# An encoder block on one core: who puts the tokens of the neighbourhood branch into column order

## The chip, the core and the metric

The kernel runs on one core of one Trainium2 chip. A core has TensorE (PE in the profile; its weight loads are the row PEld), VectorE (DVE), ScalarE (ACT), GpSimd (POOL) and SyncE (SP, which here only issues transfers). The metric is the device time of one execution in microseconds (us), lower is better.

## The reference, cut to what matters

One layer of an encoder over 1024 tokens of width 1024. The tokens are a grid of 16 rows by 64 columns, token = 64 * row + column.

```python
proj = x @ w_in + b_in                     # columns: NA q | NA k | NA v | WG q | WG k | WG v | gate_A | gate_B
ya = neighbourhood_attention(qa, ka, va)   # 8 heads of 64; a query sees an 8 x 16 window of the grid
yb = windowed_gqa(qb, kb, vb)              # 8 q heads, 2 kv heads, |t-s| <= 128
mix = sigmoid(ga) * (ya @ w_branch_a) + sigmoid(gb) * (yb @ w_branch_b)
h   = layer_norm(alpha * x + mix @ w_out)
out = layer_norm(alpha * h + expert_choice_moe(h))   # 16 SwiGLU experts, 128 tokens each
```

In row order a query's window of 16 columns is spread over the grid rows. The kernel therefore computes branch A in *column order*, token' = 16 * column + row, where a block of 128 tokens is 8 whole columns and a window lies in at most three neighbouring blocks. Everything outside branch A stays in row order.

## The kernel before, in words

Each float32 operand is split into a high part (hi, rounded to the matmul type fp32r) and the rest (lo), and a product is hi*hi + hi*lo + lo*hi. ScalarE writes the hi part, VectorE the lo part.

The stages, one after another on TensorE, whose program is in the order of the code (`manual_schedule`):

1. **Projection and attention, mixed.** `x_tile` transposes x into x^T, held in row order as `xT`. `w_in` is cut into 34 chunks of 128 columns. `proj(c, nh)` makes chunk c for one half of the tokens (nh): 24 matmuls of 128x512 into one PSUM tile `pj` (two buffers). Chunks 0 to 3 are NA q, 4 to 7 NA k, 8 to 11 NA v; 12 to 17 belong to branch B, 18 to 33 are the gates. Units of this projection wait in a list (`queue`), and `fill(n)` puts n of their matmuls between the steps of the attention (5 or 7 at a time, `FILL`, `FILA`), in an order fixed by the program. Before a unit's first matmul TensorE waits until the buffer of `pj` used two units earlier has been emptied.
2. **Branch outputs.** The attention outputs go through memory (`ya_d` in column order, `yb_d` in row order) and are loaded, split and multiplied by `w_branch_a`, `w_branch_b` in `branch(nm, d)`: 8 chunks d, two halves nh, 12 matmuls of 128x512 each for each of the two branches. The result is gated with `g_d`.
3. **Output product, LayerNorm, router and top-128 choice**, then **16 experts** whose weights are read from memory, and the last LayerNorm.

Where the order of tokens changes in the kernel before: the matmuls read x^T in row order, so `pj` is in row order, and the evictions of chunks 0 to 11 write into column order. `by_column` is the strided view (64 bytes between neighbouring columns) through which `kside` (lines 208 and 210), `qside` (217, 218) and `va_unit` (281) write; VectorE reads the hi part back through the same view. `qa_unit` needs four pieces of 64x256 for each half of tokens, since one half of the rows holds all columns. The way back is in `y_load`: for branch A the row is read through a strided view (also 64 bytes) by ScalarE (595) and VectorE (596). The functions that the change touches, with the line numbers of the profile:

Of the kernel before, what the change touches and what calls it, by code (L numbers as in the profile page):

```python
# [8 lines left out]
F32 = mybir.dt.float32  # L9
F32R = mybir.dt.float32r  # L10
I32 = mybir.dt.int32
U32 = mybir.dt.uint32
AF = mybir.ActivationFunctionType
ALU = mybir.AluOpType
# [3 lines left out]
P = 128  # L18
S = 1024
D = 1024  # L20
KD = D // P
HD = 64
GRID = 64
# [31 lines left out]
def encoder_block(ctx, tc, x, w_in, b_in, rpb, sink, w_branch_a, w_branch_b, w_out, ln1_g, ln1_b,  # L55
                  w_router, w_gate, w_up, w_down, ln2_g, ln2_b, out):
    nc = tc.nc
# [19 lines left out]
    def f32(ap):  # L77
        return ap.bitcast(F32)
# [31 lines left out]
    xp = att.enter_context(tc.tile_pool(name="xp", bufs=1))  # L110
    tbp = att.enter_context(tc.tile_pool(name="tbp", bufs=2))
    qkv = att.enter_context(tc.tile_pool(name="qkv", bufs=1))
    vtp = att.enter_context(tc.tile_pool(name="vtp", bufs=1))
    spp = att.enter_context(tc.tile_pool(name="spp", bufs=2))
    prp = att.enter_context(tc.tile_pool(name="prp", bufs=2))
    evp = att.enter_context(tc.tile_pool(name="evp", bufs=3))
    psc = att.enter_context(tc.tile_pool(name="psc", bufs=1, space=PSUM))
    ptp = att.enter_context(tc.tile_pool(name="ptp", bufs=3, space=PSUM))
    pvp = att.enter_context(tc.tile_pool(name="pvp", bufs=1, space=PSUM))
# [2 lines left out]


    xT = {}
    for h in range(2):
        for part in ("hi", "lo"):
            xT[part, h] = xp.tile([P, KD, 512], F32R, name="xT" + part + str(h))

    def x_load(t):
        xt = qkv.tile([P, D], F32, name="xt", tag="k", bufs=6)  # L130
# [3 lines left out]
    def x_tile(xt, t):  # L134
        for h in range(2):
            pt = ptp.tile([P, 4, P], F32, name="pt")
            for j in range(4):
                nc.tensor.transpose(pt[:, j, :], xt[:, (4 * h + j) * P:(4 * h + j + 1) * P], ident)
            sl = slice((t % 4) * P, (t % 4 + 1) * P)
            dst = xT["hi", t // 4][:, 4 * h:4 * h + 4, sl]  # L140
            nc.scalar.activation(dst, pt, AF.Copy)
            nc.vector.tensor_tensor(xT["lo", t // 4][:, 4 * h:4 * h + 4, sl], pt, f32(dst), op=ALU.subtract)

    held = {}
    wq, raws = [], []
# [28 lines left out]
    bcol = acp.tile([P, 34], F32, name="bcol")  # L174
    nc.vector.tensor_copy(bcol, bps[:, 0, :34])

    def proj(c, nh):
        hi, lo = held["w", c]
        ps = pp.tile([P, 512], F32, name="pj")
        n = 0  # L180
        for a, part in ((hi, "hi"), (hi, "lo"), (lo, "hi")):
            for k in range(KD):
                nc.tensor.matmul(ps, a[:, k, :], xT[part, nh][:, k, :], start=(n == 0), stop=(n == 3 * KD - 1))  # L183
                n += 1
                yield ps

# [7 lines left out]
            nc.gpsimd.dma_start(t[:, o:o + w], src)  # L194
        return t


    def by_column(ap, nh):
        return ap.rearrange("p (c r) -> p r c", r=16)[:, 8 * nh:8 * nh + 8, :]

    def by_row(ap):
        return ap.rearrange("p (r c) -> p r c", c=GRID)

    def kside(ps, c, half, khh, kll, view, src_view):
        lo, hi = half * HD, (half + 1) * HD
        src, b = src_view(ps[lo:hi]), bcol[lo:hi, c:c + 1]
        for o in (half, 1 - half):
            nc.scalar.activation(view(khh[o * HD:(o + 1) * HD]), src, AF.Identity, bias=b)
        for o in range(2):
            nc.vector.scalar_tensor_tensor(view(kll[o * HD:(o + 1) * HD]), src, b, f32(view(khh[lo:hi])),  # L210
                                           op0=ALU.add, op1=ALU.subtract)

    def qside(src, c, half, qs, view):
        lo, hi = half * HD, (half + 1) * HD
        o = 1 - half
        b = bcol[lo:hi, c:c + 1]
        nc.scalar.activation(view(qs[lo:hi]), src, AF.Identity, bias=b)
        nc.vector.scalar_tensor_tensor(view(qs[o * HD:(o + 1) * HD]), src, b, f32(view(qs[lo:hi])),
                                       op0=ALU.add, op1=ALU.subtract)

    def k_unit(key, c, nh):
        if nh == 0:
            held[key] = ([qkv.tile([P, S], F32R, name="khh", tag="k", bufs=6) for _ in range(2)],
                         [qkv.tile([P, S], F32R, name="kll", tag="k", bufs=6) for _ in range(2)])
        for ps in proj(c, nh):
            yield
        for half in range(2):
            if key == "kB":
                v, sv = lambda ap: ap[:, nh * 512:(nh + 1) * 512], lambda ap: ap
            else:  # L230
                v, sv = lambda ap: by_column(ap, nh), by_row
            kside(ps, c, half, held[key][0][half], held[key][1][half], v, sv)
        done.add((key, nh))

    def q_unit(key, c, nh):
        for ps in proj(c, nh):
            yield
        for half in range(2):
            qs = qkv.tile([P, 512], F32R, name="qs", tag="q", bufs=8)
            held.setdefault(key, {})[half, nh] = qs  # L240
            qside(ps[half * HD:(half + 1) * HD], c, half, qs, lambda ap: ap)
        done.add((key, nh))


    def qa_unit(key, c, nh):
        if nh == 0:
            held[key] = {(half, g): qkv.tile([P, 512], F32R, name="qs", tag="q", bufs=8)
                         for half in range(2) for g in range(2)}
        for ps in proj(c, nh):
            yield  # L250
        for half in range(2):
            for g in range(2):
                src = by_row(ps[half * HD:(half + 1) * HD])[:, :, 32 * g:32 * g + 32]
                qside(src, c, half, held[key][half, g], lambda ap: by_column(ap, nh))
        done.add((key, nh))

    def v_split(key, vt, j0, last):
        pt = ptp.tile([P, 4, P], F32, name="pt")
        for j in range(4):
            nc.tensor.transpose(pt[:, j, :], vt[:, (j0 + j) * P:(j0 + j + 1) * P], ident)  # L260
        v = qkv.tile([P, 4, 2, P], F32R, name="vs", tag="v", bufs=4)
        p4 = pt.rearrange("p t (h d) -> p t h d", h=2)
        nc.scalar.activation(v[:, :, :, :HD], p4, AF.Copy)
        nc.vector.tensor_tensor(v[:, :, :, HD:], p4, f32(v[:, :, :, :HD]), op=ALU.subtract)
        held.setdefault(key, []).append(v)
        done.update(last)

    def v_unit(key, c, nh):
        for ps in proj(c, nh):
            yield  # L270
        vt = evp.tile([P, 512], F32, name="vt", tag="e")
        nc.scalar.activation(vt, ps, AF.Identity, bias=bcol[:, c:c + 1])
        later.append([8, lambda: v_split(key, vt, 0, [(key, nh)])])

    def va_unit(key, c, nh):
        if nh == 0:
            held["vt", key] = vtp.tile([P, S], F32, name="vta")
        vt = held["vt", key]
        for ps in proj(c, nh):
            yield  # L280
        nc.scalar.activation(by_column(vt, nh), by_row(ps), AF.Identity, bias=bcol[:, c:c + 1])
        if nh:
            later.append([8, lambda: v_split(key, vt, 0, [(key, 0)])])
            later.append([14, lambda: v_split(key, vt, 4, [(key, 1)])])

    def g_unit(c, nh):
        for ps in proj(c, nh):
# [31 lines left out]
    def units(f, *a):  # L319
        return [(f, a + (nh,)) for nh in range(2)]  # L320

    def qkv_units(i):
        return units(qa_unit, ("q", i), i) + units(k_unit, ("k", i), 4 + i) + units(va_unit, ("v", i), 8 + i)

    gates = [u for d in range(8) for c in (18 + d, 26 + d) for u in units(g_unit, c)]

# [261 lines left out]
    def y_load(nm, src):  # L588
        for k in range(4):
            raw = gp.tile([P, S], F32, name="yraw", tag="g")  # L590
            nc.sync.dma_start(raw, src[k * P:(k + 1) * P, :])
            s0, hi, lo = raw, yT[nm][0][k], yT[nm][1][k]
            if nm == "a":
                s0, hi, lo = raw.rearrange("p (c r) -> p r c", r=16), by_row(hi), by_row(lo)
            nc.scalar.activation(hi, s0, AF.Copy)
            nc.vector.tensor_tensor(lo, s0, f32(hi), op=ALU.subtract)

    y_load("b", yb_d)
    wbr = {}
# [14 lines left out]
    def branch(nm, d):  # L614
        cs = slice((d % 2) * P, (d % 2 + 1) * P)
        g = sg[nm, d]
        for nh in range(2):
            sl = slice(nh * 512, (nh + 1) * 512)
            hi, lo = wbr[nm]
            z = zp.tile([P, 512], F32, name="z")  # L620
            n = 0
            for a, u in ((hi, 0), (lo, 0), (hi, 1)):
                for k in range(4):
                    nc.tensor.matmul(z, a[:, k, cs], yT[nm][u][k][:, sl], start=(n == 0), stop=(n == 11))
                    n += 1
            nc.vector.tensor_tensor(g[:, sl], g[:, sl], z, op=ALU.mult)
            if nm == "a":
                nc.gpsimd.tensor_tensor(g[:, sl], g[:, sl], sg["b", d][:, sl], op=ALU.add)
                nc.scalar.activation(mix[0][nh][d], g[:, sl], AF.Copy)
                nc.vector.tensor_tensor(mix[1][nh][d], g[:, sl], f32(mix[0][nh][d]), op=ALU.subtract)  # L630
# [662 lines left out]
```

## Time and profile before

| what | us |
|---|---|
| median of 3 runs | 1961.32 (1960.73 to 1965.41) |
| the profiled execution | 1960.38 |
| its span, first to last instruction | 1958.6 |
| TensorE busy | 1863.8 (95%) |
| VectorE busy | 1482.2 (76%) |
| ScalarE busy | 1222.5 (62%) |
| GpSimd busy | 221.3 (11%) |

Matmuls are pipelined, so the duration in a matmul's row is longer than what it takes of TensorE's time. What a matmul takes is the distance between the starts of neighbours. [...]

### The profile page before, as it was taken

The numbers are of one execution on the slowest core, as the hardware profiler recorded it, in microseconds if no ns is written. First come the engines' busy times: TensorE is split into PE (matmuls) and PEld (weight loads), VectorE is DVE, ScalarE is ACT, GpSimd is POOL, SyncE is SP. The second block draws the span as 40 slices with busy tenths as digits, with TensorE's granted clock in tenths as the row PEclk, the third lists the DMA queues.
The fourth block names the chain that finished last, engine by engine and source line by source line (L and its number), as shares of the span: only waits on it lengthen the run. The fifth ranks groups of instructions, "written<-read, shape, count | busy, mean of one in ns | idle before, by whom it ended". The sixth has DMA issues, their size and how long they took to land.

```text
span 1958.6 us, 23860 instructions
## 1 busy us (share of the span) xinstructions
PE 1863.8 (95%) x8795; PEld 1532.0 (78%) x8795; DVE 1482.2 (76%) x1857; ACT 1222.5 (62%) x1319; POOL 221.3 (11%) x271
## 2 busy tenths in 40 slices
PE   7998998988999999499999999999999999999996
PEld 6886877876877787388888888888888888888884
DVE  5466655554444558889989998998899899899897
ACT  4456655565444411277777777777777777777772
POOL 2121121111102222000000000000000000000003
PEclk9999999999999999699999999999999999999998
DMA  7111122222155274679999999999999999999982
GB/s 247 49 60 43 54 73 59 71 68 60 60 167 199 97 272 158 255 282 363 387 389 389 371 393 393 375 384 389 387 373 387 394 382 384 384 383 382 389 318 86
DMA packets 177129, 507.08 MB, mean 259 GB/s; under 512 B 12690, under 2 KB 55956, under 8 KB 177012
## 3 DMA queue, kind: packets, MB, share of 16 engines
q1 hardware_dynamic: 158816, 465.60, 63.5%
q0 software_dynamic: 7888, 24.13, 4.4%
q10 hardware_dynamic: 10308, 15.82, 2.4%
q8 instruction: 69, 1.13, 0.2%
q14 instruction: 48, 0.39, 0.1%
HBM read 468.40 MB, written 37.09 MB: 258 GB/s over the span
## 4 chain that ended last, share of the span: by engine, by line
PE 56%; DVE 2%; DMA 1%; issue 0%; ACT 0%; DVEq 0%; ACTq 0%
PE gu L1090 35%; PE yb L1090 18%; PE mt L1070 2%; PE gu L1098 1%; DMA xg<-h_d,idx 0%; DVE ln L1238 0%; DVE raw L1246 0%; DVE raw L1256 0%; DMA acc_d<-xr 0%; PE gu L1229 0%; PE mt L982 0%; DVE srt L752 0%; DVE srt L740 0%; DVE srt L750 0%; DVE srt L741 0%
## 5 line engine op out<-in xcount | busy, mean ns | idle before, releaser
L1053 DVE TENSOR_TENSOR mlo<-raw,mhi 128x2048 fp32r<-128x2048 f32 x383 | 859.1, 2277 | 52.8 <-PE yb L1090 26.0
L1045 ACT ACTIVATE mhi<-raw 128x2048 fp32r<-128x2048 f32 x383 | 732.3, 1912 | 200.3 <-PE gu L1090 93.7
L1090 PE MATMUL gu<-mhi,xsh 128*128 128x512 f32 x1008 | 398.2, 395 | 0.0
L1090 PE MATMUL gu<-mhi,xsl 128*128 128x512 f32 x1008 | 393.0, 390 | 0.0
L1090 PE MATMUL gu<-mlo,xsh 128*128 128x512 f32 x1008 | 393.0, 390 | 0.0
L1090 PEld LDWEIGHTS gu<-mhi,xsl 128*128 128x128 f32 x1008 | 189.5, 188 | 39.8 <-DVE xsl L1073 0.2
L1090 PEld LDWEIGHTS gu<-mlo,xsh 128*128 128x128 f32 x1008 | 189.7, 188 | 37.3
L1090 PEld LDWEIGHTS gu<-mhi,xsh 128*128 128x128 f32 x1008 | 189.6, 188 | 37.5 <-ACT xsh L1072 0.2
L1090 PE MATMUL yb<-mhi,hsl 128*128 128x512 f32 x512 | 199.4, 389 | 0.0
L1090 PE MATMUL yb<-mhi,hsh 128*128 128x512 f32 x512 | 199.3, 389 | 0.0
L1090 PE MATMUL yb<-mlo,hsh 128*128 128x512 f32 x512 | 199.2, 389 | 0.0
L183 PE MATMUL pj<-xThi,whi 128*128 128x512 f32 x544 | 157.1, 414 | 20.6 <-DVE kll L210 16.2
L183 PE MATMUL pj<-xTlo,whi 128*128 128x512 f32 x544 | 153.3, 405 | 0.0
L183 PE MATMUL pj<-xThi,wlo 128*128 128x512 f32 x544 | 151.3, 402 | 0.0
L183 PEld LDWEIGHTS pj<-xThi,whi 128*128 128x128 f32 x544 | 101.2, 195 | 43.9 <-issue 15.6
L183 PEld LDWEIGHTS pj<-xThi,wlo 128*128 128x128 f32 x544 | 99.3, 189 | 19.1
L183 PEld LDWEIGHTS pj<-xTlo,whi 128*128 128x128 f32 x544 | 98.6, 189 | 18.3
L1090 PEld LDWEIGHTS yb<-mhi,hsl 128*128 128x128 f32 x512 | 96.1, 188 | 20.0
L1090 PEld LDWEIGHTS yb<-mlo,hsh 128*128 128x128 f32 x512 | 96.1, 188 | 20.0
L1090 PEld LDWEIGHTS yb<-mhi,hsh 128*128 128x128 f32 x512 | 96.1, 188 | 19.9
L996 POOL DMA_INDIRECT xg<-h_d,idx x16 | 15.9, 993 | 810.1 <-DVE gsl L993 755.9
L1124 POOL DMA_INDIRECT acc_d<-yt,idx x15 | 39.3, 2618 | 211.3 <-ACT yt L1123 211.3
(264 smaller groups left out, 2392.6 us busy)
## 6 DMA issues: line engine op xcount, KB each, us to landing
raw<-in_w_up_dram SPq DMA_DIRECT2D x127, 1024.0 KB, 9.7
raw<-in_w_gate_dram SPq DMA_DIRECT2D x126, 1024.0 KB, 8.8
raw<-in_w_down_dram SPq DMA_DIRECT2D x126, 1024.0 KB, 9.1
wraw<-in_w_in_dram SPq DMA_DIRECT2D x34, 512.0 KB, 4.3
g_d<-gt SPq DMA_DIRECT2D x32, 256.0 KB, 2.3
sg<-g_d SPq DMA_DIRECT2D x16, 512.0 KB, 3.7
xt<-in_x_dram SPq DMA_DIRECT2D x8, 512.0 KB, 8.5
wraw<-in_w_out_dram SPq DMA_DIRECT2D x8, 512.0 KB, 5.3
```

The costliest lines, as they stand in the source:

```text
L183: nc.tensor.matmul(ps, a[:, k, :], xT[part, nh][:, k, :], start=(n == 0), stop=(n == 3 * KD - 1))
L996: nc.gpsimd.indirect_dma_start(out=xg, out_offset=None, in_=h_d, in_offset=bass.IndirectOffsetOnAxis(ap=idx[:, :1], axis=0))
L1045: nc.scalar.activation(hi[:, sl], src, AF.Copy)
L1053: nc.vector.tensor_tensor(lo[:, sl], src, f32(hi[:, sl]), op=ALU.subtract)
L1070: nc.tensor.transpose(pt[:, j, :], src[:, (4 * h + j) * P:(4 * h + j + 1) * P], ident)
L1090: nc.tensor.matmul(banks[b], a[:, k, :], ww[:, sl], start=(first and j == 0 and n == 0), stop=(last and j == len(w) - 1 and n == 2))
L1098: nc.tensor.matmul(bank, a[:, k, :], ww[:, sl], start=(k == 0 and n == 0), stop=(k == 7 and n == 2))
L1124: nc.gpsimd.indirect_dma_start(out=acc_d, out_offset=bass.IndirectOffsetOnAxis(ap=idx[:, :1], axis=0), in_=yt, in_offset=None, compute_op= ...
```

## The change

The strided access moves from ScalarE and VectorE to TensorE's moving operand. For chunks 0 to 11 `tokens` hands the matmul a view of x^T in which neighbouring elements are 64 tokens (256 bytes) apart, 32 columns of 16 rows; the PSUM tile is written contiguously and already in column order. All evictions then go without strides, and NA q, k and v use the same units as branch B. `branch("a", d)` reads y through a view with 16 elements (64 bytes) between neighbours, 8 rows of 64 columns, and `y_load` reads and writes without strides. `xT` becomes one tile per part instead of one per part and half. NA v, whose two halves shared a tile `vta`, gets a tile of the ring `evp` for each half, and this ring goes from 3 to 4 buffers. Sizes and numbers of the matmuls stay.

```diff
-    evp = att.enter_context(tc.tile_pool(name="evp", bufs=3))
+    evp = att.enter_context(tc.tile_pool(name="evp", bufs=4))
...
+    def tokens(ap, nh, grid):
+        if grid:
+            return ap.rearrange("p (r c) -> p c r", c=GRID)[:, 32 * nh:32 * nh + 32, :]
+        return ap[:, nh * 512:(nh + 1) * 512]
+
     def proj(c, nh):
         hi, lo = held["w", c]
         ps = pp.tile([P, 512], F32, name="pj")
+        po = ps.rearrange("p (c r) -> p c r", r=16) if c < 12 else ps
         n = 0
         for a, part in ((hi, "hi"), (hi, "lo"), (lo, "hi")):
             for k in range(KD):
-                nc.tensor.matmul(ps, a[:, k, :], xT[part, nh][:, k, :], start=(n == 0), stop=(n == 3 * KD - 1))
+                nc.tensor.matmul(po, a[:, k, :], tokens(xT[part][:, k, :], nh, c < 12), start=(n == 0),
+                                 stop=(n == 3 * KD - 1))
...
-    def kside(ps, c, half, khh, kll, view, src_view):
+    def kside(ps, c, half, khh, kll, sl):
         lo, hi = half * HD, (half + 1) * HD
-        src, b = src_view(ps[lo:hi]), bcol[lo:hi, c:c + 1]
+        src, b = ps[lo:hi], bcol[lo:hi, c:c + 1]
         for o in (half, 1 - half):
-            nc.scalar.activation(view(khh[o * HD:(o + 1) * HD]), src, AF.Identity, bias=b)
+            nc.scalar.activation(khh[o * HD:(o + 1) * HD, sl], src, AF.Identity, bias=b)
...
-    def va_unit(key, c, nh):
...
-        nc.scalar.activation(by_column(vt, nh), by_row(ps), AF.Identity, bias=bcol[:, c:c + 1])
-        if nh:
-            later.append([8, lambda: v_split(key, vt, 0, [(key, 0)])])
-            later.append([14, lambda: v_split(key, vt, 4, [(key, 1)])])
...
-        return units(qa_unit, ("q", i), i) + units(k_unit, ("k", i), 4 + i) + units(va_unit, ("v", i), 8 + i)
+        return units(q_unit, ("q", i), i) + units(k_unit, ("k", i), 4 + i) + units(v_unit, ("v", i), 8 + i)
...
-            if nm == "a":
-                s0, hi, lo = raw.rearrange("p (c r) -> p r c", r=16), by_row(hi), by_row(lo)
-            nc.scalar.activation(hi, s0, AF.Copy)
-            nc.vector.tensor_tensor(lo, s0, f32(hi), op=ALU.subtract)
+            nc.scalar.activation(yT[nm][0][k], raw, AF.Copy)
+            nc.vector.tensor_tensor(yT[nm][1][k], raw, f32(yT[nm][0][k]), op=ALU.subtract)
...
-                    nc.tensor.matmul(z, a[:, k, cs], yT[nm][u][k][:, sl], start=(n == 0), stop=(n == 11))
+                    y, zo = yT[nm][u][k][:, sl], z
+                    if nm == "a":
+                        y = yT[nm][u][k].rearrange("p (c r) -> p r c", r=16)[:, 8 * nh:8 * nh + 8, :]
+                        zo = z.rearrange("p (r c) -> p r c", c=GRID)
+                    nc.tensor.matmul(zo, a[:, k, cs], y, start=(n == 0), stop=(n == 11))
```

Two places show how instructions move. On ScalarE, where the q chunk of the second pair of NA heads is evicted (`qs` are the q tiles, `pTB`, `sA`, `ytmp` and `pTA` attention steps, `whi` the split of a weight chunk, `vta` the v tile), before:

```order
L217 ACTIVATE qs<-pj,bcol 64x8x32
L378 ACTIVATE pTB<-pt 128x512
L102 ACTIVATE whi<-wraw 128x1024
L394 ACTIVATE ytmp<-po 64x256
L217 ACTIVATE qs<-pj,bcol 64x8x32
L394 ACTIVATE ytmp<-po 64x256
L396 DMA yb_d<-yB 128x2x128
L217 ACTIVATE qs<-pj,bcol 64x8x32
L458 ACTIVATE pTA<-pt 128x256
L217 ACTIVATE qs<-pj,bcol 64x8x32 x2
L440 ACTIVATE sA,st<-sA,st 128x384 x3
```

and the same place after:

```order
L216 ACTIVATE qs<-pj,bcol 64x512 x2
L350 ACTIVATE pTB<-pt 128x512
L412 ACTIVATE sA,st<-sA,st 128x256
L412 ACTIVATE sA,st<-sA,st 128x384 x3
L102 ACTIVATE whi<-wraw 128x1024
L366 ACTIVATE ytmp<-po 64x256
L216 ACTIVATE qs<-pj,bcol 64x512
L366 ACTIVATE ytmp<-po 64x256
L368 DMA yb_d<-yB 128x2x128
L216 ACTIVATE qs<-pj,bcol 64x512
L430 ACTIVATE pTA<-pt 128x256
```

Four pieces for a half of the tokens become two, and the next instructions of the attention move up.

On TensorE, in the v unit of the first pair of NA heads (`pj` projection matmuls, `sc` scores, `pt<-ident,vta` the transposes of v), before:

```order
L183 MATMUL pj<-xThi_117,whi 128x512 x5
L346 MATMUL sc<-khh,qs 128x384
L346 MATMUL sc<-kll,qs 128x384
L346 MATMUL sc<-khh,qs 128x384
L346 MATMUL sc<-kll,qs 128x384
L183 MATMUL pj<-xTlo_118,whi 128x512 x5
L376 MATMUL pt<-ident,sB 128x128 x4
```

and after:

```order
L188 MATMUL pj<-xThi,whi 128x512 x5
L248 MATMUL pt<-ident,vt 128x128 x4
L318 MATMUL sc<-khh,qs 128x384
L318 MATMUL sc<-kll,qs 128x384
L318 MATMUL sc<-khh,qs 128x384
L318 MATMUL sc<-kll,qs 128x384
L188 MATMUL pj<-xTlo,whi 128x512 x5
L348 MATMUL pt<-ident,sB 128x128 x4
```

The four transposes of the first half of v come one projection unit earlier; the projection matmuls stand where they stood, with the other operand.

## Rows read from the trace of the kernel before

**Rows 1.** Stretches: window and its length, busy us (instructions) by engine, PEclk, DMA share, GB/s.
```profile
100.00:570.00 470.00, 436.96 (x2132) 359.42 (x2131) 255.09 (x602) 262.33 (x552) 80.60 (x141) 0.97 0.22 64
570.00:690.00 120.00, 113.33 (x469) 89.37 (x470) 63.24 (x74) 55.49 (x59) 26.69 (x32) 0.97 0.50 166
690.00:830.00 140.00, 110.41 (x610) 93.40 (x609) 103.18 (x399) 29.14 (x46) 22.71 (x16) 0.88 0.63 228
830.00:1958.00 1128.00, 1113.84 (x5168) 918.05 (x5166) 1009.28 (x685) 831.35 (x582) 71.47 (x43) 0.99 0.96 364
```
**Rows 2.** The costliest groups of the page, the first row of the projection.
```profile
L183 PE MATMUL pj<-xThi,whi 128*128 128x512 f32 x544 | 157.1, 414 | 20.6 <-DVE kll L210 16.2
```
**Rows 3.** Instructions of TensorE in order of time: start, us, what, count.
```profile
573.47 2.03 PE L183 MATMUL pj<-xThi,whi 128*128 128x512 f32 x8
575.34 2.03 PE L183 MATMUL pj<-xTlo,whi 128*128 128x512 f32 x8
...
586.25 1.10 PE L624 MATMUL z<-yh,whi 128*128 128x512 f32 x4
587.19 1.10 PE L624 MATMUL z<-yh,wlo 128*128 128x512 f32 x4
```
**Rows 4.** The chain that ended last, its shares by line.
```profile
PE gu L1090 35%; PE yb L1090 18%; PE mt L1070 2%; PE gu L1098 1%; DMA xg<-h_d,idx 0%; DVE ln L1238 0%; DVE raw L1246 0%; DVE raw L1256 0%; DMA acc_d<-xr 0%; PE gu L1229 0%; PE mt L982 0%; DVE srt L752 0%; DVE srt L740 0%; DVE srt L750 0%; DVE srt L741 0%
```
**Rows 5.** Groups by shape, evictions of k: first 60 us (branch B), then 150:560 (NA).
```profile
L208 ACT ACTIVATE khh<-pj,bcol 64x512 fp32r<-64x512 f32 x8 | 5.5, 684 | 4.7 <-DVE kll L210 3.1 <-PE pj L183 1.5
L210 DVE SCALAR_TENSOR_TENSOR kll<-pj,bcol,khh 64x512 fp32r<-64x512 f32 x8 | 6.0, 749 | 3.1 <-ACT khh L208 2.9
...
L208 ACT ACTIVATE khh<-pj,bcol 64x512 fp32r<-64x512 f32 x32 | 36.5, 1140 | 20.7 <-DVE kll L210 12.7 <-PE pj L183 4.7 <-DVE yA L473 2.0
L210 DVE SCALAR_TENSOR_TENSOR kll<-pj,bcol,khh 64x512 fp32r<-64x512 f32 x32 | 35.5, 1111 | 19.5 <-ACT khh L208 19.2
```
**Rows 6.** Order of time, ScalarE then VectorE: each first branch B, then A.
```profile
581.39 1.05 ACT L595 ACTIVATE yh<-yraw 128x1024 fp32r<-128x1024 f32 x1
...
584.72 1.97 ACT L595 ACTIVATE yh<-yraw 128x1024 fp32r<-128x1024 f32 x1
...
583.01 1.25 DVE L596 TENSOR_TENSOR yl<-yraw,yh 128x1024 fp32r<-128x1024 f32 x1
587.12 2.00 DVE L596 TENSOR_TENSOR yl<-yraw,yh 128x1024 fp32r<-128x1024 f32 x1
```
**Rows 7.** Groups by shape: contiguous work of 1024 and of 512 elements.
```profile
L104 DVE TENSOR_TENSOR wlo<-wraw,whi 128x1024 fp32r<-128x1024 f32 x34 | 42.3, 1245 | 20.5 <-PE pj L183 12.4 <-ACT whi L102 4.2 <-ACT sB L360 2.3
...
L102 ACT ACTIVATE whi<-wraw 128x1024 fp32r<-128x1024 f32 x34 | 36.0, 1058 | 21.8 <-PE pj L183 17.8 <-DMA wraw<-in_w_in_dram 3.6
...
L379 DVE TENSOR_TENSOR pTB<-pt,pTB 128x512 fp32r<-128x512 f32 x44 | 30.0, 689 | 18.7 <-ACT pTB L378 17.5
...
L378 ACT ACTIVATE pTB<-pt 128x512 fp32r<-128x512 f32 x44 | 25.5, 591 | 25.9 <-PE pt L376 21.2 <-DMA yb_d<-yB 2.2 <-DVE mx L348 1.6
```
**Rows 8.** Waits: who waited for whom, total us, times, longest.
```profile
PE pj L183 <- DVE kll L210: 16.2, 7, 4.5
...
PE sc L426 <- ACT khh L208: 2.9, 1, 2.9
...
PE pj L183 <- DVE qs L218: 2.5, 3, 1.4
...
PE z L624 <- ACT yh L595: 5.0, 4, 1.3
```
**Rows 9.** TensorE in order of time, around branch A's first matmuls; brackets: idle before.
```profile
591.30 0.50 PE L624 MATMUL z<-yh,whi 128*128 128x512 f32 x1 [1.33 <-ACT yh L595]
593.13 0.80 PE L624 MATMUL z<-yh,whi 128*128 128x512 f32 x1 [1.33 <-ACT yh L595]
593.73 1.91 PE L624 MATMUL z<-yh,wlo 128*128 128x512 f32 x4
595.43 1.53 PE L624 MATMUL z<-yl,whi 128*128 128x512 f32 x4
```

More of the change, by code (lines that the diff above doesn't have):

```diff
@@ L112, in encoder_block @@
     qkv = att.enter_context(tc.tile_pool(name="qkv", bufs=1))
-    vtp = att.enter_context(tc.tile_pool(name="vtp", bufs=1))
     spp = att.enter_context(tc.tile_pool(name="spp", bufs=2))
     prp = att.enter_context(tc.tile_pool(name="prp", bufs=2))
-    evp = att.enter_context(tc.tile_pool(name="evp", bufs=3))
+    evp = att.enter_context(tc.tile_pool(name="evp", bufs=4))
     psc = att.enter_context(tc.tile_pool(name="psc", bufs=1, space=PSUM))
@@ L124, in encoder_block @@
     xT = {}
-    for h in range(2):
-        for part in ("hi", "lo"):
-            xT[part, h] = xp.tile([P, KD, 512], F32R, name="xT" + part + str(h))
+    for part in ("hi", "lo"):
+        xT[part] = xp.tile([P, KD, S], F32R, name="xT" + part)
     def x_load(t):
@@ L138, in x_tile @@
                 nc.tensor.transpose(pt[:, j, :], xt[:, (4 * h + j) * P:(4 * h + j + 1) * P], ident)
-            sl = slice((t % 4) * P, (t % 4 + 1) * P)
-            dst = xT["hi", t // 4][:, 4 * h:4 * h + 4, sl]
+            sl = slice(t * P, (t + 1) * P)
+            dst = xT["hi"][:, 4 * h:4 * h + 4, sl]
             nc.scalar.activation(dst, pt, AF.Copy)
-            nc.vector.tensor_tensor(xT["lo", t // 4][:, 4 * h:4 * h + 4, sl], pt, f32(dst), op=ALU.subtract)
+            nc.vector.tensor_tensor(xT["lo"][:, 4 * h:4 * h + 4, sl], pt, f32(dst), op=ALU.subtract)
     held = {}
@@ L195, in na_table, with qside @@
         return t
[L198 to L202, printed above, removed]
-    def kside(ps, c, half, khh, kll, view, src_view):
+    def kside(ps, c, half, khh, kll, sl):
         lo, hi = half * HD, (half + 1) * HD
-        src, b = src_view(ps[lo:hi]), bcol[lo:hi, c:c + 1]
+        src, b = ps[lo:hi], bcol[lo:hi, c:c + 1]
         for o in (half, 1 - half):
-            nc.scalar.activation(view(khh[o * HD:(o + 1) * HD]), src, AF.Identity, bias=b)
+            nc.scalar.activation(khh[o * HD:(o + 1) * HD, sl], src, AF.Identity, bias=b)
         for o in range(2):
-            nc.vector.scalar_tensor_tensor(view(kll[o * HD:(o + 1) * HD]), src, b, f32(view(khh[lo:hi])),
+            nc.vector.scalar_tensor_tensor(kll[o * HD:(o + 1) * HD, sl], src, b, f32(khh[lo:hi, sl]),
                                            op0=ALU.add, op1=ALU.subtract)
-    def qside(src, c, half, qs, view):
+    def qside(ps, c, half, qs):
         lo, hi = half * HD, (half + 1) * HD
         o = 1 - half
-        b = bcol[lo:hi, c:c + 1]
-        nc.scalar.activation(view(qs[lo:hi]), src, AF.Identity, bias=b)
-        nc.vector.scalar_tensor_tensor(view(qs[o * HD:(o + 1) * HD]), src, b, f32(view(qs[lo:hi])),
+        src, b = ps[lo:hi], bcol[lo:hi, c:c + 1]
+        nc.scalar.activation(qs[lo:hi], src, AF.Identity, bias=b)
+        nc.vector.scalar_tensor_tensor(qs[o * HD:(o + 1) * HD], src, b, f32(qs[lo:hi]),
                                        op0=ALU.add, op1=ALU.subtract)
@@ L227, in k_unit @@
         for half in range(2):
[L228 to L232, printed above, removed]
+            kside(ps, c, half, held[key][0][half], held[key][1][half], slice(nh * 512, (nh + 1) * 512))
         done.add((key, nh))
@@ L240, in q_unit @@
             held.setdefault(key, {})[half, nh] = qs
-            qside(ps[half * HD:(half + 1) * HD], c, half, qs, lambda ap: ap)
+            qside(ps, c, half, qs)
         done.add((key, nh))
[L245 to L266, printed above, removed]
     def v_unit(key, c, nh):
@@ L272, in v_unit, with finish @@
         nc.scalar.activation(vt, ps, AF.Identity, bias=bcol[:, c:c + 1])
-        later.append([8, lambda: v_split(key, vt, 0, [(key, nh)])])
-    def va_unit(key, c, nh):
[L276 to L280, printed above, removed]
-        nc.scalar.activation(by_column(vt, nh), by_row(ps), AF.Identity, bias=bcol[:, c:c + 1])
-        if nh:
-            later.append([8, lambda: v_split(key, vt, 0, [(key, 0)])])
-            later.append([14, lambda: v_split(key, vt, 4, [(key, 1)])])
+        def finish():
+            pt = ptp.tile([P, 4, P], F32, name="pt")
+            for j in range(4):
+                nc.tensor.transpose(pt[:, j, :], vt[:, j * P:(j + 1) * P], ident)
+            v = qkv.tile([P, 4, 2, P], F32R, name="vs", tag="v", bufs=4)
+            p4 = pt.rearrange("p t (h d) -> p t h d", h=2)
+            nc.scalar.activation(v[:, :, :, :HD], p4, AF.Copy)
+            nc.vector.tensor_tensor(v[:, :, :, HD:], p4, f32(v[:, :, :, :HD]), op=ALU.subtract)
+            held.setdefault(key, []).append(v)
+            done.add((key, nh))
+        later.append([8, finish])
     def g_unit(c, nh):
@@ L591, in y_load @@
             nc.sync.dma_start(raw, src[k * P:(k + 1) * P, :])
-            s0, hi, lo = raw, yT[nm][0][k], yT[nm][1][k]
-            if nm == "a":
-                s0, hi, lo = raw.rearrange("p (c r) -> p r c", r=16), by_row(hi), by_row(lo)
-            nc.scalar.activation(hi, s0, AF.Copy)
-            nc.vector.tensor_tensor(lo, s0, f32(hi), op=ALU.subtract)
+            nc.scalar.activation(yT[nm][0][k], raw, AF.Copy)
+            nc.vector.tensor_tensor(yT[nm][1][k], raw, f32(yT[nm][0][k]), op=ALU.subtract)
     y_load("b", yb_d)
```

## The prediction

> **What bounds the kernel now.** I read the stretches first [rows 1]. From 100 to 570 us (projection and attention) TensorE is busy 437 of 470 us, from 570 to 690 us (branch products) 113 of 120. VectorE and ScalarE are busy about half of each. So in the two stages that the change touches TensorE is the bound, and every nanosecond added to its matmuls is on the path. The stretch from 830 us on, the experts, is TensorE as well: its matmuls at line 1090 are the two largest shares of the chain that ended last [rows 4], and nothing there is edited. It starts when the router has the last rows of h, and its first weights need only free buffers, so I let a shift of the first 690 us pass to the end one to one.
>
> What a matmul takes is read from the distance of starts [rows 3]: eight projection matmuls from 573.47 to 575.34 us, 1.87 / 8 = 0.234 us each; four of branch from 586.25 to 587.19 us, 0.235 each. The 0.4 us in a group's row [rows 2] is a pipelined duration, not a price.
>
> Last come the prices of the strided accesses of today. The same eviction of k takes ScalarE 684 ns without a stride and 1140 with one, VectorE 749 and 1111 [rows 5]. The load of y, which differs between the branches in the stride alone, takes ScalarE 1.05 and 1.97 us and VectorE 1.25 and 2.00 [rows 6].
>
> **The change part by part.**
>
> *Matmuls that now read with a stride.* Chunks 0 to 11, two halves, 24 each: 12 x 2 x 24 = 576 of the 1632 projection matmuls (three groups of 544 [rows 2], 34 chunks x 48). Branch A: 8 x 2 x 12 = 192. Together 768. Their number and size stay, and PSUM is written contiguously, so only the reading of the moving operand differs. No row of the trace shows TensorE with such a read. Lower bound: 0, since the columns stay 512 and contiguous reading can't be beaten by strided. Upper bound: the time that the two other engines need for one strided element carries over unchanged. ScalarE needs (1058 - 591) / 512 = 0.91 ns for a contiguous element, VectorE (1245 - 689) / 512 = 1.09 [rows 7]; the stride adds (1.97 - 1.05) / 1024 = 0.90 and (2.00 - 1.25) / 1024 = 0.73 ns [rows 6]. That is 1.81 and 1.82 ns, the same for two engines of different speed, which looks like a limit of the memory. At 1.8 ns a matmul takes 512 x 1.8 = 0.92 us, 0.69 more, and 768 of them 527 us more.
>
> I take the ratio instead: ScalarE's strided read of the very tile that TensorE will read, 1.97 / 1.05 = 1.88 [rows 6]. TensorE already takes a contiguous element in 0.234 / 512 = 0.46 ns, half of ScalarE's time, so its path to memory is a faster one and the absolute figure need not hold for it; that a strided element costs about twice a contiguous one is what both engines share. 0.234 x 0.88 = 0.206 us more, x 768 = 158 us (118 in the projection, 40 in branch A). With VectorE's 2.00 / 1.25 = 1.60 it is 108 us, with a plain factor of two 180.
>
> [...]
>
> *Evictions without a stride.* For one k unit (half the tokens) ScalarE falls from 4 x 1.140 = 4.6 to 4 x 0.684 = 2.7 us, VectorE from 4.4 to 3.0 [rows 5]; the four q pieces on each engine become two, and v loses its stride. Both engines have slack here, so what counts is who waited. TensorE waited 16.2 us (7 times, at most 4.5) for the lo part of k, 2.5 for that of q, 2.9 for the hi part of k [rows 8], in sum 21.6. The chain hi, then lo, gets up to 3 us shorter, and a mean wait is 16.2 / 7 = 2.3 us. If TensorE's units also get longer (24 x 0.44 = 10.6 us instead of 5.6), the emptying of the buffer is late nowhere. I take three quarters, 16 us.
>
> *Loads of y without a stride.* Of the 5.0 us that TensorE waits for the split of y [rows 8], two waits of 1.33 are for branch A [rows 9]; each load gets 0.92 us shorter [rows 6], 1.8 us. [...] Another 1 us may come back. 3 us in sum.
>
> *Clock.* In 100 to 570 us the granted clock is 0.97 [rows 1], worth 0.03 x 470 = 14 us; it falls after waits like those removed, and not only those. I take 5.
>
> *At nothing.* One tile of x^T instead of two: the first matmuls keep their place in the order. The transposes of v one unit earlier, 4 times: the waits for the v tile are no bound, and a slower projection gives them more cover. The fourth buffer of `evp`: TensorE does not wait for that ring in rows 8.
>
> *Sum.* +158 - 16 - 3 - 5 = +134. The profiled execution took 1960.4 us (span 1958.6 and 1.8 around it), which makes 2094.4; the median of the runs is 0.9 higher. I say 2095.
>
> **The rivals.**
>
> *TensorE reads strides for nothing.* Then only the savings are left. They are smaller than in the sum, since a unit still takes 5.6 us and the next one comes as early as today: of the 24 us I give 8 to 28, middle 16. Time 1945 (1933 to 1953). For it: TensorE's read is built for twice the rate of the others, and no row shows a penalty. Against it: two of two engines with a row pay. [...]
>
> *One strided element per 1.8 ns for every engine.* 1960.4 + 527 - 24 = 2463 (2390 to 2490). For it: the two equal figures of rows 6 and 7. Against it: TensorE takes contiguous elements twice as fast as ScalarE.
>
> *Part of the penalty is hidden, or only one of the two strides pays.* With branch A alone (64 bytes) paying: +40 - 24, 1977; a tenth to a half of the 158 us in general gives about 1950 to 2015.
>
> **How the numbers follow.** Twice-as-slow reads 0.36, for nothing 0.30, the 1.8 ns limit 0.24, partly hidden 0.10. The likeliest is 2095; its own range is 1960 + 108 - 24 = 2045 to 1960 + 180 - 15 = 2125. The range over the cases, 1938 to 2440, leaves out the fast edge of the free case (0.05) and a good half of the 1.8 ns case (0.14). It is wide because the one unknown price is paid 768 times. Chances by the bound of 0.3% (6 us, about what a measurement of this kernel tells from no change): faster is the free case save its weak end, 0.28; same 0.05; slower 0.67.
>
> **What would show it right or wrong.** In the profile after, the distance of starts of projection matmuls of chunks below 12 inside an undisturbed run of eight: 0.44 us by my forecast, 0.234 if strides are free, 0.92 by the third case; the gates' matmuls stay at 0.234 in each. The same for the branch products, where A and B stand side by side. Waits for `kll`, `qs` and `khh` should be nearly gone, evictions of NA k at 684 and 749 ns, loads of y at 1.05 and 1.25 us. The stretch from the first to the last expert should be as long as now, 1128 us within a few; if it grows or shrinks by more, my one-to-one shift is wrong. The forecast falls if the strided matmuls start 0.234 us apart, whatever the total does.

## The result, and the profile after

The changed kernel takes 2131.03 us (median of 4 runs, 2130.9 to 2131.4), the kernel before 1962.65 (now of 4 runs too): a ratio of 1.0857 (95% interval 1.0838 to 1.0876), 8.6% slower. The forecast was 2095 with 1938 to 2440 around it: slower was right, by about 134 us instead of the 168 measured.

The stretches of the changed kernel, cut where its stages end (columns as in [rows 1]; 100 to 694 us answers to 100 to 570 before, 694 to 858 to 570 to 690):

```profile
100.00:694.00 594.00, 589.75 (x2062) 361.01 (x2061) 230.70 (x577) 233.18 (x527) 79.60 (x140) 0.99 0.16 48
694.00:858.00 164.00, 160.76 (x535) 102.53 (x534) 68.84 (x82) 58.17 (x69) 23.37 (x32) 0.98 0.41 135
...
1000.00:2129.00 1129.00, 1114.62 (x5171) 918.65 (x5169) 1009.90 (x685) 831.83 (x583) 71.41 (x43) 0.99 0.96 364
```

The first two stretches have nearly all the loss, 758 us where they had 590, and in them TensorE has almost no idle time: 4 of 594 us, where it had 33 of 470 [rows 1]. The granted clock (PEclk, as a share of full speed) is 0.99 and 0.98 (0.97 in both before), so no lower clock explains longer matmuls. The experts take 1129 us, as before (1128).

What one matmul takes, TensorE in order of time, first in the projection, then in the branch products (start, duration, what, count):

```profile
306.32 4.42 PE L188 MATMUL pj<-xTlo,whi 128*128 128x512 f32 x8
310.54 0.73 PE L188 MATMUL pj<-xThi,wlo 128*128 128x512 f32 x1
```
```profile
740.38 1.09 PE L597 MATMUL z<-yh,whi 128*128 128x512 f32 x4
741.31 1.10 PE L597 MATMUL z<-yh,wlo 128*128 128x512 f32 x4
...
744.89 1.91 PE L597 MATMUL z<-yh,wlo 128*128 128x512 f32 x4
746.62 1.91 PE L597 MATMUL z<-yl,whi 128*128 128x512 f32 x4
```

Eight strided reads of x^T take 310.54 - 306.32 = 4.22 us, 0.528 each, against 0.234 [rows 3]. In the branch stage the contiguous products of branch B (740.38 to 741.31) take 0.233 each, the strided ones of branch A (744.89 to 746.62) 0.433. The two strides don't cost the same: 64 bytes 1.86 times a contiguous read (0.433 / 0.233), 256 bytes 2.26 times (0.528 / 0.234).

What the change was to give, it gave. Groups by shape, evictions of NA k from 150 us to the end of the stage:

```profile
L209 DVE SCALAR_TENSOR_TENSOR kll<-pj,bcol,khh 64x512 fp32r<-64x512 f32 x32 | 24.0, 750 | 12.1 <-ACT khh L207 11.8
L207 ACT ACTIVATE khh<-pj,bcol 64x512 fp32r<-64x512 f32 x32 | 22.1, 692 | 20.4 <-PE pj L188 15.7 <-DVE kll L209 4.2
```

and TensorE's waits (total us, times, longest):

```profile
PE pj L188 <- DVE kll L209: 3.2, 2, 2.9
PE z L597 <- ACT yh L564: 3.0, 3, 1.0
```

1111 and 1140 ns [rows 5] became 750 and 692; the wait for the lo part of k fell from 16.2 to 3.2 us, that for y from 5.0 to 3.0, and those for `qs` and `khh` [rows 8] are gone. All of it saves far less than the reads cost.

### The profile page after: what moved, and what is told of

Its sections match the earlier page's. It is cut to its first block, busy times and chain, and to the rows that moved or that the text cites. A ratio compares the mean times of both kernels' runs of the same rounds, so it can differ in the third digit from the quotient of the medians.

```text
span 2129.4 us, 23829 instructions
## 1 busy us (share of the span) xinstructions
PE 2068.5 (97%) x8795; PEld 1550.3 (73%) x8795; DVE 1464.0 (69%) x1841; ACT 1196.1 (56%) x1303; POOL 217.1 (10%) x271
## 4 chain that ended last, share of the span: by engine, by line
PE 92%; DVE 3%; DMA 2%; ACT 1%; issue 1%; POOL 0%; SPq 0%; DVEq 0%; ACTq 0%; POOLq 0%
PE gu L1063 32%; PE pj L188 25%; PE yb L1063 16%; PE z L597 6%; PE po L780 4%; PE mt L1043 2%; PE po L438 1%; PE sc L398 1%; PE pt L427 1%; PE sc L318 1%; PE pt L348 1%; PE po L359 1%; PE gu L1071 1%; DMA wraw<-in_w_in_dram 0%; PE pl L823 0%
## 5 line engine op out<-in xcount | busy, mean ns | idle before, releaser
L188 PE MATMUL pj<-xThi,whi 128*128 128x512 f32 x544 | 212.7, 525 | 5.0 <-DVE kll L209 3.2
L188 PE MATMUL pj<-xTlo,whi 128*128 128x512 f32 x544 | 210.6, 522 | 0.0
L188 PE MATMUL pj<-xThi,wlo 128*128 128x512 f32 x544 | 210.3, 521 | 0.0
L431 DVE TENSOR_TENSOR pTA<-pt,pTA 128x256 fp32r<-128x256 f32 (+2 forms) x80 | 35.7, 449 | 84.5 <-ACT pTA L430 83.9
```

What stands on the lines that cost most here:

```text
L188: nc.tensor.matmul(po, a[:, k, :], tokens(xT[part][:, k, :], nh, c < 12), start=(n == 0), stop=(n == 3 * KD - 1))
L431: nc.vector.tensor_tensor(pT[:, 1, at:at + m * P], ptf, f32(hi), op=ALU.subtract)
```

## The experiments

**Without the strides.** The changed kernel, with the matmuls reading contiguously. This leaves out the column order: branch A works on tokens in row order.

```diff
-        po = ps.rearrange("p (c r) -> p c r", r=16) if c < 12 else ps
+        po = ps
...
-                nc.tensor.matmul(po, a[:, k, :], tokens(xT[part][:, k, :], nh, c < 12), start=(n == 0),
+                nc.tensor.matmul(po, a[:, k, :], tokens(xT[part][:, k, :], nh, False), start=(n == 0),
...
-                    if nm == "a":
-                        y = yT[nm][u][k].rearrange("p (c r) -> p r c", r=16)[:, 8 * nh:8 * nh + 8, :]
-                        zo = z.rearrange("p (r c) -> p r c", c=GRID)
```

> The changed kernel with contiguous moving operands in both places: it leaves out the column order, so that branch A works on tokens in row order; all sizes, counts, evictions and loads are those of the changed kernel. Theory (the whole loss is the strided read: x^T 0.528 us a matmul instead of 0.234, y 0.434 instead of 0.234): 2131 - 576 x 0.294 - 192 x 0.200 = 2131 - 208 = 1923, and some 10 to 20 us of waits and clock come back since a unit of the projection is short again: 1933 to 1945, about 20 us faster than the kernel before. Rival (the new order of evictions, the later tiles or the buffers cost something of their own): 1960 or more.

Measured: 1929.44 us, a ratio of 0.9826 (0.981 to 0.9843) to the kernel before at 1962.18. It is a little faster than the 1933 to 1945 expected. So the strided reads alone cost 2131.0 - 1929.4 = 202 us, and all the rest of the change saves 33. The rival, a cost in the new order or the later tiles that eats up the savings, is out. TensorE's waits in this kernel:

```profile
PE z L594 <- ACT yh L564: 5.0, 5, 1.6
PE pj L188 <- DVE kll L209: 3.8, 3, 2.9
```

Most of the wait for k goes without any help from longer matmuls: shorter evictions do it. Other waits stay longer than in the changed kernel, that for y at 5.0 us against 3.0; the part on the savings comes back to this.

**Branch part alone.** The kernel before with y loaded without strides and read by TensorE 64 bytes apart.

```diff
...
-                    nc.tensor.matmul(z, a[:, k, cs], yT[nm][u][k][:, sl], start=(n == 0), stop=(n == 11))
+                    y, zo = yT[nm][u][k][:, sl], z
+                    if nm == "a":
+                        y = yT[nm][u][k].rearrange("p (c r) -> p r c", r=16)[:, 8 * nh:8 * nh + 8, :]
+                        zo = z.rearrange("p (r c) -> p r c", c=GRID)
+                    nc.tensor.matmul(zo, a[:, k, cs], y, start=(n == 0), stop=(n == 11))
```

> The kernel before with only the branch part of the change: y of branch A is loaded without strides and read by TensorE with 64 bytes between elements; x^T as before. Theory (read price of the profile after): 192 x 0.200 = 38 more, 2 to 3 us of waits for y less: 1961 + 36 = 1997. Rival (the branch stage has slack that hides a part, or the stage's end is set by others): 1965 to 1980.

Measured: 1993.3 us, ratio 1.0156 (1.0139 to 1.0173), 31 us more (27 to 34). That is a little under the 36 expected and above the 4 to 19 of the rival: slack in the stage hides at most a small part.

**Projection part alone.** The changed kernel with `y_load` and `branch` as they were before.

```diff
...
-                    y, zo = yT[nm][u][k][:, sl], z
-                    if nm == "a":
-                        y = yT[nm][u][k].rearrange("p (c r) -> p r c", r=16)[:, 8 * nh:8 * nh + 8, :]
-                        zo = z.rearrange("p (r c) -> p r c", c=GRID)
-                    nc.tensor.matmul(zo, a[:, k, cs], y, start=(n == 0), stop=(n == 11))
+                    nc.tensor.matmul(z, a[:, k, cs], yT[nm][u][k][:, sl], start=(n == 0), stop=(n == 11))
```

> The changed kernel with the branch part of the kernel before: only x^T is read with strides. Theory: 2131 - 38 + 3 = 2096, that is 1961 + 169 - 34. Rival (the two parts help each other's clock or waits, so they don't add up): off by more than 6 us from 2096.

Measured: 2098.97 us, ratio 1.0696 (1.0678 to 1.0714), 137 us more, 3 above the 2096 expected. 31 + 137 = 168 is the whole loss: the parts add up.

**A pattern for each chunk.** The changed kernel, where chunks 0 to 11 read x^T through views of their own on lines of their own. What branch A computes then has no meaning.

```diff
-                nc.tensor.matmul(po, a[:, k, :], tokens(xT[part][:, k, :], nh, c < 12), start=(n == 0),
-                                 stop=(n == 3 * KD - 1))
+                x, w, f = xT[part][:, k, :], a[:, k, :], dict(start=(n == 0), stop=(n == 3 * KD - 1))
+                if c in STEP:                      # {1: 2, 2: 4, 3: 8, 4: 16, 5: 32, 6: 64}
+                    m = STEP[c] // 2
+                    x = x.rearrange("p (r c) -> p c r", c=STEP[c])[:, m * nh:m * nh + m, :]
...
+                elif c in RUN:                     # {9: 2, 10: 4, 11: 16}
+                    g = 32 // RUN[c]
+                    x = x.rearrange("p (r g u) -> p g r u", g=2 * g, u=RUN[c])[:, g * nh:g * nh + g]
...
+                if c == 0:
+                    nc.tensor.matmul(o, w, x, **f)
...
```

> The changed kernel in which each of the chunks 0 to 11 reads x^T through a view of its own, on a line of its own (what branch A computes has no meaning): contiguous; one element every 8, 16, 32, 64, 128 and 256 bytes (chunks 1 to 6); 64 bytes in 32 runs of 16 elements (7); 256 bytes in 4 runs of 128 (8); 2, 4 and 16 neighbours together every 256 bytes (9 to 11). Always 512 columns. Theory A (the distance between neighbours sets the price): chunk 7 starts every 0.434 us like y, chunk 8 every 0.528 like x^T, chunk 11 close to 0.234. Theory B (the short runs of 16 set the extra price of x^T): chunk 7 every 0.528, chunk 8 0.43 or less, chunk 11 about 0.33. [...]

One execution, 2063.7 us. The mean durations by line, of the hi*hi products alone. A duration is longer than the distance of starts by a part that differs little between rows (412 ns against 0.234 us when contiguous, about 0.64 against 0.45 at 8 bytes), so a price is read, to within some 0.04 us, by subtracting the contiguous row:

```profile
L224 PE MATMUL pj<-xThi,whi 128*128 128x512 f32 x16 | 10.1, 770 | 0.0
L220 PE MATMUL pj<-xThi,whi 128*128 128x512 f32 x16 | 9.5, 743 | 0.0
L226 PE MATMUL pj<-xThi,whi 128*128 128x512 f32 x16 | 9.4, 736 | 0.0
L212 PE MATMUL pj<-xThi,whi 128*128 128x512 f32 x16 | 8.1, 655 | 0.0
L210 PE MATMUL pj<-xThi,whi 128*128 128x512 f32 x16 | 8.1, 644 | 0.0
L216 PE MATMUL pj<-xThi,whi 128*128 128x512 f32 x16 | 7.8, 628 | 0.0
L218 PE MATMUL pj<-xThi,whi 128*128 128x512 f32 x16 | 7.7, 622 | 0.0
L214 PE MATMUL pj<-xThi,whi 128*128 128x512 f32 x16 | 7.7, 621 | 0.0
L222 PE MATMUL pj<-xThi,whi 128*128 128x512 f32 x16 | 7.6, 617 | 0.0
L228 PE MATMUL pj<-xThi,whi 128*128 128x512 f32 x16 | 5.2, 456 | 0.0
L208 PE MATMUL pj<-xThi,whi 128*128 128x512 f32 x16 | 5.0, 412 | 0.0
L230 PE MATMUL pj<-xThi,whi 128*128 128x512 f32 x16 | 4.6, 412 | 0.0
```

and starts inside undisturbed runs, at 64 and at 8 bytes, (167.57 - 164.50) / 7 = 0.439 and (288.65 - 285.03) / 8 = 0.453 us apart:

```profile
164.50 3.27 PE L216 MATMUL pj<-xThi,whi 128*128 128x512 f32 x7
167.57 1.49 PE L216 MATMUL pj<-xTlo,whi 128*128 128x512 f32 x3
...
285.03 3.82 PE L210 MATMUL pj<-xTlo,whi 128*128 128x512 f32 x8
288.65 2.46 PE L210 MATMUL pj<-xThi,wlo 128*128 128x512 f32 x5
```

| line | one element, or run, every | mean ns |
|---|---|---|
| 208 | contiguous | 412 |
| 210, 212 | 8 bytes, 16 bytes | 644, 655 |
| 214, 218 | 32 bytes, 128 bytes | 621, 622 |
| 216 | 64 bytes, 8 runs of 64 | 628 |
| 222 | 64 bytes, 32 runs of 16 | 617 |
| 220 | 256 bytes, 32 runs of 16 | 743 |
| 224 | 256 bytes, 4 runs of 128 | 770 |
| 226, 228, 230 | 2, 4, 16 neighbours every 256 bytes | 736, 456, 412 |

Theory A holds for its three chunks: going from 64 to 256 bytes raises the price, from 628 to 743 ns, and short runs of 16 do not (617 beside 628; 4 long runs at 256 bytes, 770, are no cheaper than 32 short ones). Theory B is out. Two neighbours every 256 bytes cost as much as one (736 and 743). The price begins at once, at a distance of two elements (644 against 412), and does not grow from there to 128 bytes (622); four neighbours are read nearly as fast as contiguous data (456 against 412), and no pattern is read faster.

**The extra of 256 bytes.** The same means, with distances around 256 bytes, each in 8 runs of 64, and two kinds of runs of 8.

```diff
...
+                if c in STEP:            # {0: 64, 1: 65, 2: 66, 3: 68, 4: 72, 5: 80, 6: 96, 7: 128, 8: 48}
+                    g = 8 * ((k + 4 * nh) % (STEP[c] // 8))
+                    x = xT[part].rearrange("p k s -> p (k s)")[:, :64 * STEP[c]]
+                    x = x.rearrange("p (r c) -> p c r", c=STEP[c])[:, g:g + 8, :]
...
+                elif c == 9:
+                    x = x.rearrange("p (r g u) -> p g r u", g=8, u=8)[:, 4 * nh:4 * nh + 4]
...
```

> The changed kernel with one view of x^T per chunk again (what branch A computes has no meaning): one element every 64, 65, 66, 68, 72, 80, 96, 128 and 48 elements of 4 bytes (chunks 0 to 8), each in 8 runs of 64; runs of 8 neighbours every 256 bytes, as in the kernel with blocks of 8 for x^T (9) and every 512 bytes as there for y (10); contiguous (11). Theory A (256 bytes and its multiples meet the same part of the memory again and cost extra): chunks 0 and 7 at 0.53 us and more, all other strides at 0.434. Theory B (the price grows with the distance itself): 65 to 96 all above 0.50, 48 between. Chunks 9 and 10: 0.25 to 0.27 each if the jump alone costs.

One execution, 2062.2 us, again the hi*hi products. Lines 203 to 217 are 64, 65, 66, 68, 72, 80, 96 and 128 elements in this order, 219 is 48, 221 and 223 are runs of 8 every 256 and every 512 bytes, 225 is contiguous:

```profile
L203 PE MATMUL pj<-xThi,whi 128*128 128x512 f32 x16 | 10.3, 770 | 0.0
L217 PE MATMUL pj<-xThi,whi 128*128 128x512 f32 x16 | 9.7, 765 | 0.0
L205 PE MATMUL pj<-xThi,whi 128*128 128x512 f32 x16 | 8.6, 681 | 0.0
L209 PE MATMUL pj<-xThi,whi 128*128 128x512 f32 x16 | 8.2, 652 | 0.0
L207 PE MATMUL pj<-xThi,whi 128*128 128x512 f32 x16 | 8.0, 647 | 0.0
L219 PE MATMUL pj<-xThi,whi 128*128 128x512 f32 x16 | 8.0, 626 | 0.0
L211 PE MATMUL pj<-xThi,whi 128*128 128x512 f32 x16 | 7.7, 622 | 0.0
L213 PE MATMUL pj<-xThi,whi 128*128 128x512 f32 x16 | 7.7, 623 | 0.0
L215 PE MATMUL pj<-xThi,whi 128*128 128x512 f32 x16 | 7.7, 616 | 0.0
L221 PE MATMUL pj<-xThi,whi 128*128 128x512 f32 x16 | 5.1, 442 | 0.0
L223 PE MATMUL pj<-xThi,whi 128*128 128x512 f32 x16 | 4.7, 426 | 0.0
L225 PE MATMUL pj<-xThi,whi 128*128 128x512 f32 x16 | 4.5, 406 | 0.0
```

256 and 512 bytes cost 770 and 765 ns, while 192, 288, 320 and 384 bytes cost 616 to 626 like 64: the extra belongs to 256 and its double, not to far distances. Theory A holds with a softer edge than expected: 260, 264 and 272 bytes lie between (681, 647, 652). What in the memory makes it so was not tried. Runs of 8 neighbours cost 36 and 20 ns over contiguous (442 and 426 against 406), as expected for the jump alone.

**A version that uses this: 8 columns together.** The changed kernel with the order (column / 8, row, column % 8). A block of 128 tokens still holds 8 whole columns, so the attention stays as it is; TensorE reads runs of 8 neighbours, and the bias tables are laid out for that order at the start.

```diff
...
-            return ap.rearrange("p (r c) -> p c r", c=GRID)[:, 32 * nh:32 * nh + 32, :]
+            return ap.rearrange("p (r g u) -> p g r u", g=8, u=8)[:, 4 * nh:4 * nh + 4]
...
-                        y = yT[nm][u][k].rearrange("p (c r) -> p r c", r=16)[:, 8 * nh:8 * nh + 8, :]
-                        zo = z.rearrange("p (r c) -> p r c", c=GRID)
+                        y = yT[nm][u][k].rearrange("p (g r u) -> p r g u", g=8, u=8)[:, 8 * nh:8 * nh + 8]
+                        zo = z.rearrange("p (r g u) -> p r g u", g=8, u=8)
...
+    for kind, src in enumerate((near, full)):
+        tb = prp.tile([P, 8, TW], F32, name="rpt", tag="pt")
+        for u in range(8):
+            for g in range(3):
+                nc.gpsimd.tensor_scalar(tb[:, u, P * g:P * g + P].rearrange("p (r u) -> p r u", u=8),
+                                        src[:, :, 7 - u + 8 * g:15 - u + 8 * g], 8.0, 1.0, op0=ALU.mult, op1=ALU.mult)
+        nc.gpsimd.dma_start(rp_d[kind].rearrange("c r h x -> (r h) c x"), tb)
```

> The changed kernel with another order inside branch A's blocks of 128 tokens: 8 columns together, (column / 8, row, column % 8) instead of (column, row). TensorE then reads x^T and y in runs of 8 neighbours (32 bytes), and the bias tables are laid out anew for it (48 small copies on GpSimd at the start, 1536 bytes a row in memory). The pattern runs gave 0.28 us a matmul for runs of 4 and 0.256 for runs of 16, where contiguous ones of the same run took 0.234 to 0.255. Theory (the price is paid per jump between runs that leave a line, evictions are free of strides as in the kernel without strides, 1929): 768 x 0.01 to 0.03 = 8 to 23 us over 1929, so 1937 to 1952, faster than both kernels. Rival (a jump of 256 or 512 bytes costs more than the run saves, or the tables' work at the start is on the path): 1960 or more.

Measured: 1946.2 us over 6 runs, the kernel before 1959.8; ratio 0.992 (0.9901 to 0.9939). It is faster than both kernels, than the kernel before by little but clear of the noise. Each set against the kernel before as it was timed beside it, this one is 13.6 us faster and the kernel without strides 32.7: 19 us lie between them, 0.025 us a matmul. The rows above give (442 - 406) ns x 576 + (426 - 406) x 192 = 25 us, a little more than measured. The theory lays the price on jumps that leave a line; no run shows such a line. What the runs show is a price by the length of the run: 736 ns for 2 neighbours every 256 bytes, 456 for 4, 442 for 8 (where contiguous took 406), 412 for 16. The tables' copies on GpSimd

```profile
19.65 8.83 POOL L493 TENSOR_SCALAR rpt<-rp 128x128 f32<-128x128 f32 x24
28.52 0.99 POOL L495 DMA_DIRECT2D rp_d<-rpt  x1
29.58 9.21 POOL L493 TENSOR_SCALAR rpt<-rp 128x128 f32<-128x128 f32 x23
```

lie before 40 us, while the first block's projection runs, and delay nothing that shows: of the first 100 us TensorE is busy 92.25, and 91.77 in the kernel without strides.

## Why the prediction was right, and where its sizes were off

**Where the loss is.** TensorE is the bound in the two stages, and what is added to its matmuls is on the path: right. 0.294 x 576 + 0.199 x 192 = 169 + 38 = 207 us by the rows after; the kernel without strides puts it at 202, which is net of waits that the longer matmuls cover (see the savings).

**One to one to the end.** Right: the experts' first matmul moved from 829.5 to 1000.4 us, the last from 1888.2 to 2059.1, both by 170.9, and the span grew by 170.8, between the two profiled executions (before, then after):

```profile
L1090 PE MATMUL gu<-mhi,xsh x1008: 389/389/792, 829.5 to 1888.2; 128*128 128x512 f32 x168
L1063 PE MATMUL gu<-mhi,xsh x1008: 389/389/793, 1000.4 to 2059.1; 128*128 128x512 f32 x168
```

**The price of the branch reads.** 40 us forecast, 38 by the rows. The ratio of ScalarE's strided read of the same tile, 1.88, met TensorE's 0.433 / 0.234 = 1.85. No run shows why these two should agree; VectorE's ratio, 1.60, would have missed. That "about double" carried over is the part that was argued, the close match is luck.

**The price of the x^T reads.** This is the term that was mis-sized: 118 us forecast, 169 measured. The step took the ratio of a read 64 bytes apart and used it for one 256 bytes apart. No row before had that distance as a read, and the pattern runs show that 256 bytes is a bad one: 743 to 770 ns where 64 or 320 take 617 to 628.

**The savings.** 24 us forecast, 33 measured by the kernel without strides, and 39 in the changed kernel itself: 207 us of dearer reads, and a whole time only 168 us longer. The pages split it (TensorE's line, changed kernel, then without strides; the kernel before was busy 1863.8 of 1958.6 us):

```profile
PE 2068.5 (97%) x8795; PEld 1550.3 (73%) x8795; DVE 1464.0 (69%) x1841; ACT 1196.1 (56%) x1303; POOL 217.1 (10%) x271
PE 1858.2 (96%) x8795; PEld 1529.5 (79%) x8795; DVE 1459.3 (76%) x1841; ACT 1191.4 (62%) x1303; POOL 221.3 (11%) x271
```

What is left of the span is TensorE's idle time: 94.8 us before, 60.9 in the changed kernel (span 2129.4), 70.3 without strides (span 1928.5). So the changed kernel is busy 204.7 us longer and idle 33.9 us shorter, which is the 170.8 of the span. The term for the clock fits: 5 us and 1 forecast, and without strides the same matmuls keep TensorE busy 5.6 us less (mean granted clock 0.983 against 0.980). Stretches before, after TensorE's waits of 4.54 and 3.57 us for the lo part of k and after the second wait for y, then one after the change, after a wait of 0.97 us for y (columns as in [rows 1]):

```profile
331.00:333.00 2.00, 2.00 (x8) 1.71 (x7) 0.00 (x0) 0.00 (x0) 0.00 (x0) 0.50 0.32 73
402.00:408.00 6.00, 4.84 (x15) 4.36 (x16) 3.57 (x6) 3.33 (x3) 0.00 (x0) 0.50 0.31 87
593.73:595.43 1.70, 1.70 (x5) 1.32 (x4) 1.69 (x1) 0.35 (x2) 0.00 (x0) 0.50 0.60 241
...
728.40:733.00 4.60, 4.60 (x11) 3.08 (x12) 2.21 (x3) 2.12 (x2) 0.00 (x0) 0.63 0.81 259
```

The clock was 0.50 there, and 0.63 in the last. No run shows the 1 us by itself: the four matmuls from 593.73 us took 0.425 us each, 0.8 us in all over 0.234, and the clock still falls at that place after the change. The waits were sized too low: 18 us forecast (16 for k and q, 2 for y), 34 gained. The waits that I named gave 20 of them (21.6 + 5.0 us before, 3.2 + 3.0 after); the others I had left out, most of all that of the transposes for GpSimd (before, changed kernel, without strides):

```profile
PE pt L376 <- POOL sB L365: 6.2, 8, 3.8
PE pt L348 <- POOL sB L337: 0.9, 4, 0.2
PE pt L348 <- POOL sB L337: 3.7, 7, 2.4
```

These waits are also why the rival in which strides cost nothing was set too high: 1945 forecast, 1929 measured. Its reason, that short units keep a part of the waits, holds in the sum though not for k (3.8 us without strides, 3.2 with): 9.4 us of the idle time are back when the reads are cheap, and I had given 8.

**The total.** The reads were forecast 49 us too cheap and the savings 15 us too small. That one miss took back a part of the other, and left 2095 within 36 us of 2131, is luck.

**The rivals.** Reads for nothing: out, by 0.433 and 0.528 us. One element per 1.8 ns for every engine: out, that would be 0.92 us; the equal figures of ScalarE and VectorE were no common limit for TensorE. Only one stride pays: out, since each part costs time when it stands alone. Partly hidden: out, since TensorE's busy time grew by 204.7 us, nearly the 207 of the rows, and the span by just that less the idle time gained.

**Where the price begins.** A distance of 2 elements already costs 644 against 412 ns, two neighbours every 256 bytes cost 736, as much as one (743), and four cost 456. In distances of starts, 512 contiguous columns take 0.234 us, and 0.43 and more with a stride. Why it begins at two elements, no run shows.

## What to carry to other kernels

Before a stride is handed to the engine that bounds a stage, find what that engine pays for it: here a strided access took ScalarE and VectorE 1.5 to 1.9 times as long and TensorE 1.9 to 2.3 times, and 33 us of TensorE's waits and clock were bought with 202 us of its matmuls. If an order has to change on the way through TensorE, keep at least four, better eight, float32 neighbours together (44 ns, and 20 to 36, over contiguous here), and where single elements must be read, avoid steps of 256 bytes (743 to 770 ns, where 64 bytes took 617 to 628): choosing an equally valid order inside the block turned 8.6% slower into 0.8% faster. A ratio read from one distance is no price for another until a run has shown it.

## What the runs showed of the hardware that was not expected

- TensorE's moving operand of 512 fp32r elements reads at about half rate from a distance of two elements on: starts 0.43 to 0.46 us apart for 8 to 128 bytes, against 0.234 contiguous, at a mean granted clock of 0.98.
- 256 and 512 bytes are dearer than any other distance tried (765 to 770 ns against 616 to 626 for 192, 288, 320 and 384 bytes, in runs of 64), with a fade-out at 260 to 272 (681 to 647). Why is open.
- Groups of 4 neighbours, 16 bytes, cost 44 ns over contiguous, of 8 20 to 36 ns, of 16 nothing that shows in these rows (412 against 412); pairs cost as much as single elements (736 and 743 ns).
